# The recurrent branch's output product by Strassen's algorithm, in two groups of two pairs

## The chip, the cores and the metric

One core of a Trainium2 chip runs the kernel. The metric is the device time of one execution in microseconds (us): of three runs before the change the median is 1410.3, the lowest 1408.74 and the highest 1410.36. Engines are named as in the profile: PE (TensorE, matmuls), DVE (VectorE), ACT (ScalarE), POOL (GpSimd), SP (the queue that issues most loads).

## The reference

A decoder layer on 1024 tokens of 1024 channels in float32. Two mixers read one normalised input through one projection `z = u @ w_in`; their outputs are gated per channel and merged, and one more projection follows. The part around the change:

```python
y_pool = causal_multiscale_pool(z_pool, pool_w[i], pool_scale[i]) @ pool_proj[i]      # 512 -> 1024
y_lru = rglru_branch(z_lru, z_gelu, ...) @ lru_proj[i]                                # 1024 -> 1024
gates = jax.nn.sigmoid(z_gate.reshape(B, S, N_BRANCHES, D_MODEL) + b_gate[i])
merged = gates[:, :, 0, :] * y_pool + gates[:, :, 1, :] * y_lru
h = h + merged @ w_out[i]
```

Behind it come a SwiGLU block (`w_ffn_in`, `w_ffn_out`), a gated embedding and a last norm.

## The kernel before, in words

Everything is kept transposed: a tile has 128 channels on the partitions and 1024 tokens along the row, and a tensor of 1024 channels is eight such tiles. All stay in one pool of 51 buffers of SBUF (`at`, tag "a"); what doesn't fit goes through DRAM and comes back (`spill`, `store` on the POOL queue, loads on SP).

*Precision.* A float32 operand is made of two parts, a high one that ACT casts (`hi`, L115) and the low rest that DVE subtracts (`lo`, L119), each 128x512. A product of two operands takes three matmuls: high x high, high x low, low x high. `mm3` (L215) does this for one bank of 512 tokens, `mm6` (L223) for both banks of 1024 tokens with one weight.

*Two ways to multiply.* `plain` (L840) takes a block of 128 output channels after another: per output tile eight blocks of 128 inputs, two banks, three matmuls, 48 in all, in units of four input blocks (24 matmuls). `strassen` (L419) takes the output tiles in pairs and halves both the tokens and the channels: seven products of a pair (`PRODUCT`, L50, in the order `QS`, L417), each a unit of four input blocks by three matmuls (12), on sums of weights (`PairOf.operand`, L187: S1 to S4, DVE at L194) and on sums of activations (`Acts.run`, L386: operands B11, T1, T2, B21, T3, B22, T4 of each pair of input tiles; differences on DVE at L400 to L406). `Plain` (L484) adds the products of a pair up into two tiles z: ACT copies those of 1, 5, 6 and 4, DVE adds 2, 7 and 3. The input projection and the SwiGLU block's two products go by `strassen` before the change, the other products by `plain`.

*Order.* All engines follow the order in which the program is written. `drive` (L276) goes through the units: it runs the drain of the unit before (`post`), prepares weights three units ahead (cast, then low half), calls the unit's `pre`, lets `run_background` (L242) do some of the waiting generators (two at a time, by rough costs that they yield), and emits the unit's matmuls. What is written later on an engine waits behind what is written earlier.

*The stages here.* Pooling's product (`w_pproj`, four input blocks, 24 matmuls a tile) starts when the last tile of the recurrent branch, `y`, is stored; its drain `done_pproj` (L910) multiplies the first gate into each of eight tiles `t0`, which stay in SBUF. Beside it each of the eight y tiles comes back from DRAM and is split into operands (`reload`, L880). Then the recurrent product (`w_lru`, `plain` with the first two tiles' halves interleaved): `done_lru` (L930) multiplies the second gate into a tile, adds `t0` and splits the sum into operands `m`, one tile after every 48 matmuls. The output projection (`w_out`) follows, with the first norm's spreading (L367) ahead of it.

Of the kernel before, what the change touches and what calls it, by code (L numbers as in the profile page):

```python
# [19 lines left out]
KD = D // P  # L20
# [5 lines left out]
NH = 8  # L26
# [38 lines left out]
def hybrid_block(ctx: ExitStack, tc: tile.TileContext, xT, pT, vec, w_in, w_rgig, w_pool,  # L65
                 w_pproj, w_lru, w_out, w_fin, w_fout, w_pg, w_pp, outT):
    nc = tc.nc
# [8 lines left out]
    def at(name, dt=F32):  # L76
        return ap_.tile([P, T], dt, name=name, tag="a", bufs=NA)
# [4 lines left out]
    def spill(name):  # L82
        return dp.tile([P, T], F32, name=name, tag=name)
# [3 lines left out]
    def store(out, x):  # L87
        pool.dma_start(out, x)
# [32 lines left out]
    def split(x, name):  # L121

        ops = at(name, F32R), at(name, F32R)
        for op, s in zip(ops, (LOW, HIGH)):
            hi(op, x[:, s])
        for op, s in zip(ops, (LOW, HIGH)):
            lo(op, x[:, s])
        return ops
# [128 lines left out]
    def force(*keys):  # L257

        while any(k not in have for k in keys):
            assert background or inserted, keys  # L260
            for g in list(background)[:2]:
                step(g)
            while inserted:
                u = inserted.popleft()
                u.emit()
                u.post()
# [606 lines left out]
    t0 = {}  # L873
    gate_of = {}

    def load_gate(i):
        gate_of[i] = at("g")
        nc.sync.dma_start(gate_of[i], g_spill[i])

    def reload(src, into, key, name):  # L880
        x = at(name)
        nc.sync.dma_start(x, src)
        yield None
        yield None
        ops = into[key] = at(name, F32R), at(name, F32R)
        hi(ops[0], x[:, LOW])
        hi(ops[1], x[:, HIGH])
        yield None
        lo(ops[0], x[:, LOW])
        lo(ops[1], x[:, HIGH])  # L890
        have.add((name, "op", key))
        yield 1.4

    def begin_mixed():

        while "free" not in have or any(("mx", g) not in have for g in range(NG)):
            yield None
        for gi in range(NG):
            background.append(reload(m_spill[gi], mixed, gi, "mx"))
        load_gate(0)  # L900

    def pre_pproj(m, a):
        if m == 0:
            force(*[("y", c) for c in range(NH)], *[("mx", "op", g) for g in range(NG)])
            for c in range(NH):
                background.append(reload(y_spill[c], ys, c, "y"))
        if m + 1 < KD:
            load_gate(m + 1)

    def done_pproj(m, banks):  # L910
        g = gate_of.pop(m)
        for b, s in zip(banks, (LOW, HIGH)):
            dve.tensor_mul(g[:, s], g[:, s], b)
        t0[m] = g

    plain([w_pproj[m] for m in range(KD)], NG, lambda: mixed, done_pproj, pre_pproj)


    ms = {}

    def pre_lru(m, a):
        if m == 0 and a == 0:
            force(*[("y", "op", c) for c in range(4)])
            load_gate(8)
        if m == 0 and a == 4:
            force(*[("y", "op", c) for c in range(4, NH)])
        if a == 0 and m + 1 < KD:
            load_gate(8 + m + 1)

    def done_lru(m, banks):  # L930
        g = gate_of.pop(8 + m)
        for b, s in zip(banks, (LOW, HIGH)):
            dve.tensor_mul(g[:, s], g[:, s], b)
        dve.tensor_add(g, g, t0.pop(m))
        ms[m] = split(g, "m")

    plain([w_lru[m] for m in range(KD)], KD, lambda: ys, done_lru, pre_lru, 2)


    h_spill = [spill(f"h{m}") for m in range(KD)]  # L940
# [33 lines left out]
                state["norm2"] = Rstd(state["ss2"])  # L974
        return then

    plain([w_out[m] for m in range(KD)], KD, lambda: ms, lambda m, banks: residual(m)(banks), pre_out, 2)


    f_spill = [spill(f"f{j}") for j in range(NJ)]  # L980
# [207 lines left out]
    for p, s in enumerate((LOW, HIGH)):  # L1188
        for m in range(KD - NHOLD, KD):
# [27 lines left out]
            def pre(p=p, m=m):  # L1217
                if p == 0 and m + 1 < KD:
                    load_e(m + 1)
# [55 lines left out]
```

## Time and profile before

| | |
|---|---|
| median of three runs | 1410.3 us |
| the profiled execution's own time | 1409.52 us |
| its span | 1407.8 us |
| TensorE's mean granted clock in it | 0.986 |
| TensorE, VectorE, ScalarE, GpSimd busy | 97, 73, 48, 6% of the span |

The span runs from the first to the last instruction; the execution's own time adds what lies around it. Shares are averages over all stages; where a stage's limit lies is read from the rows of that stage.

### The profile page before, as it was taken

The page shows a single profiled execution, that of the slowest core. Times are in us where ns is not written, and L with a number is a line of the kernel's source. Part 1 is how long each engine was busy: PE and PEld are TensorE (multiplying, and loading weights), DVE is VectorE, ACT ScalarE, POOL GpSimd, SP SyncE. Part 2 cuts the span into 40 slices and gives each one's busy share as a digit, 9 for nine tenths or more (in the row PEclk, how much of TensorE's full clock was granted, in tenths as well). Part 3 has the DMA queues.
Part 4 walks back from the last instruction along what each step waited for, and adds up shares of the span by engine and source line. Part 5 has one row for each costly group of instructions (what it writes and reads, how often), then busy time and mean ns, then how long its engine had stood idle before and what let it go on. Part 6 is the DMA issues. An engine that isn't in the chain of part 4 may idle for free.

```text
span 1407.8 us, 16468 instructions
## 1 busy us (share of the span) xinstructions
PE 1364.6 (97%) x6006; PEld 1121.5 (80%) x6006; DVE 1032.6 (73%) x1523; ACT 675.3 (48%) x1074; POOL 86.5 (6%) x194
## 2 busy tenths in 40 slices
PE   6999999999999999999999999999999999999986
PEld 4787888888788888888888888888888877887865
DVE  5977788888785544566798888888878767768566
ACT  6558665887867112323554444444454422126331
POOL 0003010010000000000001000010110100000000
PEclk8999999999999999999999999999999999999997
DMA  7122143332549224231134334444577798813203
GB/s 315 75 79 95 61 155 111 115 134 99 200 162 400 89 75 147 105 125 43 60 115 152 132 143 148 150 149 165 194 266 269 295 419 303 326 64 120 72 19 120
DMA packets 64737, 220.55 MB, mean 157 GB/s; under 512 B 7312, under 2 KB 9872, under 8 KB 64656
## 3 DMA queue, kind: packets, MB, share of 16 engines
q1 hardware_dynamic: 45936, 151.80, 30.2%
q0 software_dynamic: 18576, 67.64, 11.9%
q8 instruction: 47, 0.77, 0.2%
q14 instruction: 34, 0.28, 0.1%
q10 hardware_dynamic: 144, 0.06, 0.0%
HBM read 147.65 MB, written 71.83 MB: 156 GB/s over the span
## 4 chain that ended last, share of the span: by engine, by line
PE 85%; DVE 6%; ACT 4%; issue 3%; DMA 1%; POOL 1%; DVEq 0%; SPq 0%; ACTq 0%; POOLq 0%
PE ps L221 22%; PE ps L219 22%; PE ps L220 22%; PE ps L227 17%; DVE w L119 1%; DVE ss L328 1%; DMA lT<-fT 1%; PE ps L367 1%; PE ps L345 1%; DVE pg L1139 0%; ACT pg L1137 0%; DVE h L1140 0%; ACT sq L1145 0%; DVE pg L1136 0%; DMA x<-xT 0%
## 5 line engine op out<-in xcount | busy, mean ns | idle before, releaser
L115 ACT CAST w<-wr 128x512 fp32r<-128x512 f32 (+2 forms) x376 | 221.6, 608 | 339.9 <-DVE wr L194 245.0
L119 DVE TENSOR_TENSOR w<-wr,w 128x512 fp32r<-128x512 f32 (+2 forms) x376 | 249.9, 671 | 44.2 <-ACT w L115 43.4
L221 PE MATMUL ps<-xT,w 128*128 128x512 f32 x640 | 249.5, 390 | 1.5 <-DVE w L119 1.4
L219 PE MATMUL ps<-xT,w 128*128 128x512 f32 x640 | 249.4, 390 | 0.1
L220 PE MATMUL ps<-xT,w 128*128 128x512 f32 x640 | 249.1, 389 | 0.0
L219 PE MATMUL ps<-xB,w 128*128 128x512 f32 x480 | 187.2, 390 | 2.1 <-ACT xB L115 1.2
L220 PE MATMUL ps<-xB,w 128*128 128x512 f32 x480 | 187.4, 391 | 1.9 <-DVE xB L119 1.9
L221 PE MATMUL ps<-xB,w 128*128 128x512 f32 x480 | 187.4, 390 | 0.0
L221 PEld LDWEIGHTS ps<-xT,w 128*128 128x128 f32 x640 | 120.1, 188 | 28.1 <-DVE w L119 3.2
L219 PEld LDWEIGHTS ps<-xT,w 128*128 128x128 f32 x640 | 120.2, 188 | 25.1 <-ACT w L115 0.5
L220 PEld LDWEIGHTS ps<-xT,w 128*128 128x128 f32 x640 | 120.1, 188 | 25.1
L220 PEld LDWEIGHTS ps<-xB,w 128*128 128x128 f32 x480 | 90.3, 188 | 21.8 <-DVE xB L119 3.1
L219 PEld LDWEIGHTS ps<-xB,w 128*128 128x128 f32 x480 | 90.2, 188 | 21.5 <-ACT xB L115 1.6
L221 PEld LDWEIGHTS ps<-xB,w 128*128 128x128 f32 x480 | 90.3, 188 | 19.2 <-DVE w L119 0.6
L227 PE MATMUL ps<-m,w 128*128 128x512 f32 x384 | 87.3, 389 | 0.0
L227 PE MATMUL ps<-y,w 128*128 128x512 f32 x384 | 87.2, 389 | 0.0
L227 PEld LDWEIGHTS ps<-y,w 128*128 128x128 f32 x384 | 72.1, 188 | 15.0
L227 PEld LDWEIGHTS ps<-m,w 128*128 128x128 f32 x384 | 72.0, 188 | 14.9
L1068 DVE TENSOR_TENSOR h<-h,ps 128x512 f32<-128x512 f32 x68 | 46.5, 684 | 42.5 <-PE ps L221 42.4
L194 DVE TENSOR_TENSOR wr<-wr 128x512 f32<-128x512 f32 (+1 forms) x104 | 70.4, 678 | 3.0 <-DMA wr<-w_fout 1.2
L219 PE MATMUL ps<-lT,w 128*128 128x512 f32 x176 | 69.0, 392 | 3.4 <-DMA lT<-fT 2.7
L221 PE MATMUL ps<-lT,w 128*128 128x512 f32 x176 | 68.7, 390 | 0.0
(214 smaller groups left out, 2190.3 us busy)
## 6 DMA issues: line engine op xcount, KB each, us to landing
wr<-w_fin SPq DMA_DIRECT2D x44, 512.0 KB, 5.6
fT<-xT POOLq DMA_DIRECT2D x44, 512.0 KB, 5.0
lT<-fT SPq DMA_DIRECT2D x44, 512.0 KB, 7.9
wr<-w_in SPq DMA_DIRECT2D x36, 512.0 KB, 4.3
fB<-xB POOLq DMA_DIRECT2D x33, 512.0 KB, 5.8
lB<-fB SPq DMA_DIRECT2D x33, 512.0 KB, 6.7
g<-z POOLq DMA_DIRECT2D x16, 512.0 KB, 2.9
g<-g SPq DMA_DIRECT2D x16, 512.0 KB, 6.4
```

The lines of the kernel that those rows point to most:

```text
L115: act.copy(op[:, :x.shape[1]], x)
L119: dve.tensor_tensor(op[:, H:H + n], x, op[:, :n].bitcast(F32), ALU.subtract)
L194: f(self.place(out), self.place(a), self.place(b))
L219: pe.matmul(bank, a, xop[:, :H], start=first, stop=False, skip_group_check=more)
L220: pe.matmul(bank, a, xop[:, H:], start=False, stop=False, skip_group_check=more)
L221: pe.matmul(bank, b, xop[:, :H], start=False, stop=last, skip_group_check=more)
L227: pe.matmul(bank, w, xop[:, s], start=f, stop=e)
L328: dve.tensor_add(ss, ss, sq)
L345: pe.matmul(m[:, i:i + 1], self.ss[:, t:t + P], mean, start=True, stop=last is None)
L367: pe.matmul(bank[:, i * P:(i + 1) * P], r[:, b + i:b + i + 1].broadcast_to([P, P]), ident, start=True, stop=True)
L1068: dve.tensor_add(h[t][:, s], h[t][:, s], bank)
```

## The change

- The recurrent product goes by `strassen`, four pairs of output tiles in two groups of two, with the weights' rows paired on the host (`pairs`).
- y comes back in pairs of tiles (`reload_pair`), and five of its seven operands are made in the background, beside pooling's product; B22 and T4 are made in the first group by `prepare_y`.
- Pooling's gated tiles are stored to DRAM (`t_spill`) and loaded again, with the second gates, at the third to sixth product of each group (`gates_of_group`).
- `merge` multiplies the gate into the whole tile z, adds t and splits the sum. It runs as soon as a pair's tile is complete: after its product 3 for the even tile, after its product 4 for the odd one.
- `w_out` takes its inputs in the order 0, 1, 2, 3, 4, 6, 5, 7.

```diff
@@ -891,6 +891,17 @@
         have.add((name, "op", key))
         yield 1.4
 
+    ya = Acts()
+
+    def reload_pair(k):
+        t = at("y"), at("y")
+        for i in (0, 1):
+            nc.sync.dma_start(t[i], y_spill[2 * k + i])
+        yield None
+        yield None
+        ya.a[k], ya.b[k] = t
+        yield from some_operands(ya, k, ORDER[:5])
+
     def begin_mixed():
 
         while "free" not in have or any(("mx", g) not in have for g in range(NG)):
@@ -902,8 +913,8 @@
     def pre_pproj(m, a):
         if m == 0:
             force(*[("y", c) for c in range(NH)], *[("mx", "op", g) for g in range(NG)])
-            for c in range(NH):
-                background.append(reload(y_spill[c], ys, c, "y"))
+            for k in range(NH // 2):
+                background.append(reload_pair(k))
         if m + 1 < KD:
             load_gate(m + 1)
 
@@ -911,30 +922,44 @@
         g = gate_of.pop(m)
         for b, s in zip(banks, (LOW, HIGH)):
             dve.tensor_mul(g[:, s], g[:, s], b)
-        t0[m] = g
+        store(t_spill[m], g)
+
+    t_spill = [spill(f"t{m}") for m in range(KD)]
 
     plain([w_pproj[m] for m in range(KD)], NG, lambda: mixed, done_pproj, pre_pproj)
 
 
     ms = {}
 
-    def pre_lru(m, a):
-        if m == 0 and a == 0:
-            force(*[("y", "op", c) for c in range(4)])
-            load_gate(8)
-        if m == 0 and a == 4:
-            force(*[("y", "op", c) for c in range(4, NH)])
-        if a == 0 and m + 1 < KD:
-            load_gate(8 + m + 1)
-
-    def done_lru(m, banks):
-        g = gate_of.pop(8 + m)
-        for b, s in zip(banks, (LOW, HIGH)):
-            dve.tensor_mul(g[:, s], g[:, s], b)
-        dve.tensor_add(g, g, t0.pop(m))
-        ms[m] = split(g, "m")
-
-    plain([w_lru[m] for m in range(KD)], KD, lambda: ys, done_lru, pre_lru, 2)
+    prepare_y = prepare(ya)
+
+    def gates_of_group(m0):
+        def pre(q, j, size):
+            i = QS.index(q)
+            if m0 == 0:
+                if i == 0 and j == 0:
+                    while len(ya.b) < NH // 2:
+                        for g in list(background)[:2]:
+                            step(g)
+                prepare_y(q, j, size)
+            if j == 0 and i in (2, 3, 4, 5):
+                m = m0 + {2: 0, 3: 2, 4: 1, 5: 3}[i]
+                load_gate(8 + m)
+                t0[m] = at("t")
+                nc.sync.dma_start(t0[m], t_spill[m])
+        return pre
+
+    def merge(m):
+        def then(z):
+            g = gate_of.pop(8 + m)
+            dve.tensor_mul(g, g, z)
+            dve.tensor_add(g, g, t0.pop(m))
+            ms[m] = split(g, "m")
+        return then
+
+    strassen(ya, [(w_lru[2 * i], w_lru[2 * i + 1]) for i in range(KD // 2)],
+             lambda i: Plain(merge(2 * i), merge(2 * i + 1)), gates_of_group(0),
+             last=gates_of_group(4), groups=[2, 2])
 
 
     h_spill = [spill(f"h{m}") for m in range(KD)]
@@ -974,7 +999,8 @@
                 state["norm2"] = Rstd(state["ss2"])
         return then
 
-    plain([w_out[m] for m in range(KD)], KD, lambda: ms, lambda m, banks: residual(m)(banks), pre_out, 2)
+    plain([w_out[m] for m in range(KD)], KD, lambda: ms, lambda m, banks: residual(m)(banks), pre_out, 2,
+          (0, 1, 2, 3, 4, 6, 5, 7))
 
 
     f_spill = [spill(f"f{j}") for j in range(NJ)]
@@ -1256,7 +1282,7 @@
-        "w_lru": tiles(a["lru_proj"][0]),
+        "w_lru": tiles(pairs(a["lru_proj"][0])),
```

Three places of the order. In the names, xB and xT are operands of y, w a weight's operand, wr the weight as loaded (its sums are made in place), s the sum S2, z a product's tile, g a gate, t pooling's gated tile, m an operand of `w_out`.

VectorE at the seam, before: the last drain of pooling's product, the rest of y's low halves, the first drain of the recurrent product.

```order
L913 TENSOR_TENSOR g<-g,ps 128x512 x2
L119 TENSOR_TENSOR w<-wr,w 128x512 x2
L119 TENSOR_TENSOR y<-y 128x512 x4
L119 TENSOR_TENSOR w<-wr,w 128x512
L119 TENSOR_TENSOR y<-y 128x512 x4
L933 TENSOR_TENSOR g<-g,ps 128x512 x2
L934 TENSOR_TENSOR g<-g 128x1024
L119 TENSOR_TENSOR m<-g,m 128x512 x2
L119 TENSOR_TENSOR w<-wr,w 128x512
```

The first multiply of the merge (L933) has only y's low halves and weights ahead of it. VectorE there now, from the same last drain; the first xB in these rows belongs to the third pair of y.

```order
L924 TENSOR_TENSOR g<-g,ps 128x512 x2
L119 TENSOR_TENSOR w<-wr,w 128x512
L194 TENSOR_TENSOR s_3929<-wr 128x512
L119 TENSOR_TENSOR xT_3895<-y,xT_3895 128x512
L119 TENSOR_TENSOR xT_3897<-y,xT_3897 128x512
L119 TENSOR_TENSOR xB_3943<-y,xB_3943 128x512
L119 TENSOR_TENSOR xB_3945<-y,xB_3945 128x512
L400 TENSOR_TENSOR y<-y 128x512
L119 TENSOR_TENSOR w<-s_3929,w 128x512
L194 TENSOR_TENSOR s_3929<-wr 128x512
L400 TENSOR_TENSOR y<-y 128x512
L119 TENSOR_TENSOR xT_3950<-y,xT_3950 128x512
```

Where eight plain low halves of y followed the drain, S2's difference and the operands of a product now do; the third and fourth B11 (the two xB) stand behind the last drain and behind S2's difference. ScalarE at the same place, its casts of these operands:

```order
L115 CAST xT_3897<-y 128x512
L115 CAST w<-s_3929 128x512
L115 CAST xB_3943<-y 128x512
L115 CAST xB_3945<-y 128x512
L115 CAST xT_3950<-y 128x512
L497 COPY z<-ps 128x512
```

S2's cast, which reads the difference, has come to stand ahead of the casts of the third and fourth B11.

VectorE at the end of the first group: from the differences of T4 to the third merge.

```order
L406 TENSOR_TENSOR y<-y 128x512 x2
L119 TENSOR_TENSOR xT_4183<-y,xT_4183 128x512
L406 TENSOR_TENSOR y<-y 128x512
L503 TENSOR_TENSOR z<-z,ps 128x512
L955 TENSOR_TENSOR g<-g,z 128x1024
L956 TENSOR_TENSOR g<-g,t 128x1024
L119 TENSOR_TENSOR m<-g,m 128x512 x2
L119 TENSOR_TENSOR w<-wr,w 128x512
L119 TENSOR_TENSOR xT_4186<-y,xT_4186 128x512
L406 TENSOR_TENSOR y<-y 128x512
L119 TENSOR_TENSOR xT_4190<-y,xT_4190 128x512
L119 TENSOR_TENSOR xT_4224<-y,xT_4224 128x512
```

The first merge (L955, L956, m) stands ahead of T4's last three operands.

VectorE behind it, from the second merge to the third and the low half of a weight:

```order
L503 TENSOR_TENSOR z<-z,ps 128x512
L955 TENSOR_TENSOR g<-g,z 128x1024
L956 TENSOR_TENSOR g<-g,t 128x1024
L119 TENSOR_TENSOR m<-g,m 128x512 x2
L119 TENSOR_TENSOR w<-wr,w 128x512
L194 TENSOR_TENSOR wr<-wr 128x512 x2
L955 TENSOR_TENSOR g<-g,z 128x1024
L956 TENSOR_TENSOR g<-g,t 128x1024
L119 TENSOR_TENSOR m<-g,m 128x512 x2
L119 TENSOR_TENSOR w<-wr,w 128x512
```

One weight's low half and one weight's two sums now stand between two merges; before, 48 matmuls of TensorE lay between two. ScalarE at the same place, in its casts of m and of weights:

```order
L115 CAST m<-g 128x512 x2
L115 CAST w<-wr 128x512
L509 COPY z<-ps 128x512
L115 CAST m<-g 128x512 x2
L115 CAST w<-wr 128x512
L509 COPY z<-ps 128x512
L115 CAST m<-g 128x512 x2
```

The cast of the weight's sum stands ahead of the copy of product 4 (L509), and that copy ahead of the cast of m.

## Rows read from the trace of the kernel before

**Rows 1.** The page's first lines: busy us (share of the span) and instructions.

```profile
span 1407.8 us, 16468 instructions
...
PE 1364.6 (97%) x6006; PEld 1121.5 (80%) x6006; DVE 1032.6 (73%) x1523; ACT 675.3 (48%) x1074; POOL 86.5 (6%) x194
```

**Rows 2.** Chain that ended last, 380 to 700 us: start us, us, what.

```profile
429.03 130.56 PE ps L227 x576
559.59 1.78 PE ps L367 x16
561.38 87.08 PE ps L227 x384
```

**Rows 3.** By stage: busy us of PE, PEld, DVE, ACT, POOL; clock, DMA share, GB/s.

```profile
385.00:425.00 40.00, 39.63 (x175) 32.58 (x174) 30.15 (x45) 27.14 (x43) 1.59 (x3) 1.00 0.53 186
429.00:472.60 43.60, 43.60 (x194) 36.10 (x193) 24.78 (x37) 24.24 (x38) 2.23 (x5) 1.00 0.70 276
472.60:559.60 87.00, 87.00 (x386) 72.06 (x385) 42.32 (x62) 14.77 (x27) 0.00 (x0) 1.00 0.32 109
```

**Rows 4.** Waits, 420 to 660 us: us in total, times, longest us.

```profile
DVE g L933 <- PE ps L227: 39.4, 8, 8.4
```

**Rows 5.** Timeline of VectorE, 470 to 494 us: start us, us, operation, [idle before].

```profile
472.37 1.28 DVE L913 TENSOR_TENSOR g<-g,ps 128x512 f32<-128x512 f32 x2 [3.56 <-PE ps L227]
473.57 1.29 DVE L119 TENSOR_TENSOR w<-wr,w 128x512 fp32r<-128x512 f32 x2
474.77 2.49 DVE L119 TENSOR_TENSOR y<-y 128x512 fp32r<-128x512 f32 x4
477.18 0.68 DVE L119 TENSOR_TENSOR w<-wr,w 128x512 fp32r<-128x512 f32 x1
...
488.69 1.28 DVE L933 TENSOR_TENSOR g<-g,ps 128x512 f32<-128x512 f32 x2 [8.42 <-PE ps L227]
490.00 1.23 DVE L934 TENSOR_TENSOR g<-g 128x1024 f32<-128x1024 f32 x1
491.97 1.29 DVE L119 TENSOR_TENSOR m<-g,m 128x512 fp32r<-128x512 f32 x2 [0.74 <-ACT m L115]
493.18 0.69 DVE L119 TENSOR_TENSOR w<-wr,w 128x512 fp32r<-128x512 f32 x1
```

**Rows 6.** Timeline of ScalarE, pieces from 425 to 500 us.

```profile
434.71 0.58 ACT L509 COPY z<-ps 128x512 f32<-128x512 f32 x1
...
440.11 2.17 ACT L115 CAST y<-y 128x512 fp32r<-128x512 f32 x4
...
491.32 1.15 ACT L115 CAST m<-g 128x512 fp32r<-128x512 f32 x2 [22.41 <-DVE g L934]
492.37 0.62 ACT L115 CAST w<-wr 128x512 fp32r<-128x512 f32 x1
```

**Rows 7.** As rows 3, of stretches in and after stops of TensorE.

```profile
36.00:40.00 4.00, 2.18 (x7) 1.23 (x8) 3.86 (x6) 1.24 (x2) 0.00 (x0) 1.00 0.32 131
40.00:44.00 4.00, 4.00 (x12) 3.09 (x12) 3.93 (x7) 0.62 (x1) 0.00 (x0) 0.58 0.00 0
1390.00:1392.00 2.00, 0.00 (x0) 0.00 (x0) 1.38 (x2) 0.53 (x1) 0.00 (x0) 0.92 0.00 0
1392.00:1394.00 2.00, 1.24 (x6) 1.25 (x7) 0.00 (x0) 1.91 (x2) 0.00 (x0) 0.50 0.00 0
```

**Rows 8.** Chain that ended last, 36 to 46 us.

```profile
39.75 0.62 PE ps L220
40.37 0.43 PE ps L221
...
43.66 0.23 PE ps L220
```

**Rows 9.** DMA issues: operation, count, KB each, median us to landing.

```profile
g<-z POOLq DMA_DIRECT2D x16, 512.0 KB, 2.9
g<-g SPq DMA_DIRECT2D x16, 512.0 KB, 6.4
...
wr<-w_lru SPq DMA_DIRECT2D x8, 512.0 KB, 6.9
```

## Prediction

> **What bounds the kernel now.** I read the page's busy times first: TensorE is busy for 1364.6 of 1407.8 us, VectorE for 1032.6 [rows 1]. The reader should not stop there, since 97% is an average. Next comes the chain that ended last, from pooling's product on: 576 matmuls follow each other without a piece between them, 130.56 us, so **0.2267 us for one**, then 1.78 us of the norm's spreading, then 384 more [rows 2]. Of these 576, 192 are pooling's product (429.0 to 472.6 us) and 384 the recurrent branch's (472.6 to 559.6). By stage, TensorE is busy in every microsecond of both; VectorE has 24.78 of 43.6 and 42.32 of 87.0 us to do, ScalarE 24.24 and 14.77 [rows 3]. The waits agree: the drains of the recurrent product wait for TensorE, 39.4 us in eight times [rows 4]. So TensorE bounds this place, and VectorE has about half its time free. A matmul saved here is worth 0.2267 us as long as VectorE stays ahead of TensorE, and that is what the change uses up.
>
> **Prices.** A VectorE operation on 128x512 (call it a half) takes 0.68 us alone, 0.60 in a row: four take 2.49 [rows 5]. One on 128x1024 takes 1.23 and starts 0.03 after the one whose result it reads [rows 5]. A ScalarE cast takes 0.62, 0.52 in a row (four: 2.17), a copy from a bank 0.58 [rows 6]. The turn from VectorE to ScalarE and back costs VectorE 0.74 us of idleness at every merged tile [rows 5], for the cast starts 0.09 us behind the sum (490.00 + 1.23, then 491.32) and lasts 0.62 [rows 5, 6].
>
> **What is removed.** Four pairs of output tiles by seven products of 4 x 3 matmuls are 336 instead of 384: 48 x 0.2267 = **10.9 us less** on TensorE, all of it on the path. The Trainium skill (TensorE: Matmul & The Clock Gate, Back-to-back issue gap) gives about 131 ns for a 512-column matmul in a sustained stream; by that the saving would be 6.3 us. The trace disagrees with it, 0.2267 us here, and the row decides.
>
> **What is added.** VectorE gets 60 instructions more: 44 instead of 16 for the operands of y (per pair of tiles seven low halves and four differences), 44 instead of 16 for the weights, and 28 instead of 24 in the drains and merges. That is 28 + 28 halves and 7.2 us of wider drains, about 41 us of work. Pooling's product covers 14 halves of y and four differences of weights, 10.8 us, where eight halves of y stood: 24.78 + 6.0 us in 43.6. This costs nothing; without that cover it would stand ahead of the first product. The other 35 us come on top of 42.32 in a stage that should last 28 units of 12 matmuls, 76.2 us: by the sum alone VectorE is full there, so it matters where its queue is late.
>
> *The seam.* The third and fourth operand B11 stand in VectorE's queue behind the last drain of pooling's product, which can't start before 472.37 [rows 5]. Behind it come two drains, one weight half and the difference S2: 3 x 0.60 + 0.68 = 2.48, so 474.85. ScalarE casts S2 first (0.09 + 0.52) and then the third B11 (0.62): 476.1. VectorE subtracts: 476.8, and the fourth 477.4. TensorE started the first product at 472.6 and wants their low halves with its 8th and 11th matmul, at 474.2 and 474.9. It stops for **2.6 us** in all. Before, the second four tiles of y had two units of 24 matmuls between the seam and their use.
>
> *The merges of the first group.* This is the larger stop. From the end of the 11th of the 28 units (the first S4 product, 12 matmuls or 2.72 us each) VectorE's queue holds, in this order: the drain of the first tile and its merge, a weight, the rest of operand T4, drain and merge of the second tile, a weight and two differences, the third merge, a weight and two differences, the fourth merge, and the low half of the second S1. Priced:
> - a merge: 1.26 + 1.23 + 0.74 + 1.20 = 4.43; before, the like took 488.69 to 493.18, 4.49 [rows 5]; two of the four have a drain of 0.71 ahead: 4 x 4.43 + 1.42 = 19.1
> - the rest of T4, four halves of which the last waits for a difference and its cast: 0.60 + 1.42 + 0.60 = 2.6
> - the weight 0.60; then twice a weight, two differences of which the second reads the first, and a turn by ScalarE that casts the weight and only then copies the bank that the next merge reads: 0.60 + 0.71 + 0.68 + 0.09 + 0.52 + 0.65 = 3.25, so 6.5
> - the last low half 0.68
>
> In all 29.5 us. It starts 1.5 us behind the unit's end, since 4.2 us of such work stand behind the unit before. TensorE has 6 units and 2 matmuls to do meanwhile, 16.8 us, and then needs that last low half. So it waits 29.5 + 1.5 - 16.8, **14.2 us**, in three stops: on T4's last three operands (5 us), the first S1's low half (4), the second's (5).
>
> *After that* VectorE recovers. The last group has the same four merges, with four weights 21.5 us from its S4 product's end; but w_out takes the eighth tile 3 units, 1.8 us of spreading and 15 us of its own matmuls later, 25 us. Hidden, and the new order of w_out's sum gives the tiles in the order in which they are made.
>
> *The clock.* The trace shows what a stop can do: between 36 and 40 us TensorE is busy 2.18 of 4 us, and in the next four the granted clock is 0.58; near the end it is idle from 1390 to 1392 and then at 0.50, the 1.2 GHz level [rows 7]. In the first of these places nine steps took 39.75 to 43.66, 3.91 us where 2.04 would do: 1.9 us lost [rows 8]. The last two stops are 4 and 5 us with 2.3 us of work between. I take one fall, **1.9 us**, behind the last stop; falls at the earlier ones only shorten the stop after them, since VectorE sets its end. Bounds: 0, and two that count, 3.8.
>
> *Transfers.* Eight stores of 0.5 MB join the POOL queue beside pooling's product and eight loads the SP queue. Gate and t tile of the first merge are asked for six units, 16 us, ahead of their use; a gate lands in 6.4 us, weights of this product in 6.9, a stored gate in 2.9 [rows 9], and the DMA engines are at 0.32 in that stage [rows 3]. Nothing, then; the upper bound is one landing of 6.9 that is not covered, as behind the SP queue's load of t2, which waits for the store of t7 with the second group's weights behind it. ScalarE's 40 added casts and copies, 21 us, fit beside its 14.77 of 87.
>
> **Sum.** -10.9 + 2.6 + 14.2 + 1.9 = **+7.8 us**. The profiled execution took 1409.52 us around its span of 1407.8; the median of the runs, 1410.3, is 0.8 above it. On the median: **1418.1**. With the seam at 2.1 to 3.1, the chain 1.5 us either way and the clock at 0 to 3.8, the case itself reaches from +3.9 to +11.7: 1414.2 to 1422.0.
>
> The Trainium skill (VectorE: DVE Perf Modes, The DRAIN you can't avoid) says that the next operation doesn't start until the pipeline has emptied. By that each half would cost 0.68 and the chain some 1.5 us more, 1419.6. The trace has 2.49 for four, so the row's 0.60 stands.
>
> **Rivals.**
> 1. *VectorE runs the merges without gaps* (not slower). The same instructions at their pace in a row, eight wide ones at 1.20 and 22 halves at 0.60, are 22.8 instead of 29.5 us; TensorE then waits 7.5, its gaps are short and the clock stays, and the sum is -10.9 + 2.6 + 7.5 = -0.8: 1409.5. The point is a chain of 23.6 us. For it: in the input projection, also by Strassen's algorithm, VectorE is 30.15 of 40 us busy and TensorE hardly misses a beat, 39.63 [rows 3]. Against it: the idle 0.74 us stand in the trace inside each merge [rows 5]. 0.14.
> 2. *The stops are only the seam's*: VectorE comes to the first merge so far ahead, 14 us, that the merges pass while TensorE works. -10.9 + 2.6: 1402.0. The input projection speaks for it as well; but no merge stands in its stream, and VectorE can't be ahead of a product that it drains. 0.05.
> 3. *The clock doesn't fall*: +5.9, 1416.2. For it: between 36 and 40 us it still stands at 1.00 with TensorE idle for nearly half the time [rows 7]. 0.18.
> 4. *A transfer is late on top*, 6.9: 1425.0. 0.05.
>
> My forecast has 0.58. The range takes the case's own bounds and reaches down to the first rival, 1409.4 to 1422.0, which leaves out rivals 2 and 4, 0.10. About 0.2%, 2.8 us, is what a measurement can tell from no change. Slower by more: 0.58 + 0.18 + 0.05 = 0.81; within: most of rival 1, 0.09; faster: rival 2 and the rest of 1, 0.10.
>
> **What would show it.** Right: TensorE has three idle places of 4 to 5 us in the second half of this stage, ended by VectorE (an operand T4, then weights of line 119), and one of some 2 us at its start; the stage lasts about 95 us instead of 87; the clock is below 1.00 in it once; w_out's stage is as long as before. Wrong: a stage of 76 to 80 us; or waits there that a DMA ends; or time lost outside it.

## The result, and the profile after

The changed kernel takes **1419.24 us** (median of four runs, 1418.91 to 1420.89) beside 1410.33 of the kernel before on the same chip: a ratio of 1.0059, 95% interval 1.0044 to 1.0075, **8.9 us slower** by the medians (their quotient is 1.0063, inside the interval). The profiled execution took 1418.91 us around a span of 1416.8. The forecast was 1418.1 in a range of 1409.4 to 1422.0.

The page's first lines answer to [rows 1]: 48 matmuls fewer, 60 VectorE instructions more.

```profile
span 1416.8 us, 16536 instructions
...
PE 1360.5 (96%) x5958; PEld 1115.2 (79%) x5958; DVE 1075.1 (76%) x1583; ACT 697.8 (49%) x1114; POOL 91.0 (6%) x202
```

TensorE saves only 4.1 us of busy time, where 48 x 0.2267 are 10.9: a matmul at the lower clock counts as busy for longer (0.63 us instead of 0.39 from 477.66 to 480.22 us, with starts 0.427 us apart instead of 0.2267). The chain that ended last, behind the stage, answers to [rows 2]:

```profile
569.70 1.78 PE ps L367 x16
571.49 87.08 PE ps L227 x384
```

The spreading (L367) started at 559.59 before and now at 569.70; `w_out`'s 384 matmuls last 87.08 us in both. From pooling's first matmul (428.87 before, 429.19 now) to the spreading it was 130.72 us and is 140.51: **9.8 us more in this stage**. What lies behind it takes 848.2 us before and 847.1 now, a difference that two executions of one kernel show as well (the repeat of the changed kernel, below, has 848.7). The stage in two windows, columns as in [rows 3]:

```profile
429.40:472.90 43.50, 43.50 (x193) 36.03 (x192) 30.83 (x47) 19.43 (x29) 5.96 (x12) 1.00 0.79 321
472.90:569.70 96.80, 83.71 (x338) 66.78 (x338) 71.57 (x104) 37.61 (x68) 0.53 (x1) 0.93 0.44 153
```

Pooling's product covers 6.05 us more of VectorE's work (30.83, it was 24.78) and costs TensorE nothing: 43.50 of 43.50. The recurrent product lasts 96.80 us. Its 336 matmuls would take 336 x 0.2267 = 76.2; so 20.6 us are lost: 13.1 of stops (96.80 less 83.71) and 7.5 with TensorE busy for longer than its matmuls need at 0.2267. Most of the 7.5 is the lower clock (mean 0.93 of full speed). Some is not: with the clock at 1.00 throughout, the same product still keeps TensorE busy for 77.68 us (experiment 5). TensorE's waits from 460 to 580 us name the stops (us in total, times, longest):

```profile
PE ps L221 <- DVE w L119: 6.3, 2, 3.3
PE ps L220 <- DVE xT L119: 4.4, 1, 4.4
PE ps L219 <- ACT xB L115: 2.2, 1, 2.2
PE ps L220 <- DVE xB L119: 0.2, 1, 0.2
```

The two xB are the third and fourth operand B11 at the seam, xT is operand T4, and w are the two weights S1 of the second group, 3.3 and 3.0 us. No stop is ended by a DMA. VectorE's timeline shows what stood ahead of T4 and of S1 (start us, us, operation, [idle before]):

```profile
508.99 0.68 DVE L503 TENSOR_TENSOR z<-z,ps 128x512 f32<-128x512 f32 x1
509.70 1.22 DVE L955 TENSOR_TENSOR g<-g,z 128x1024 f32<-128x1024 f32 x1
510.96 1.23 DVE L956 TENSOR_TENSOR g<-g,t 128x1024 f32<-128x1024 f32 x1
512.87 1.29 DVE L119 TENSOR_TENSOR m<-g,m 128x512 fp32r<-128x512 f32 x2 [0.68 <-ACT m L115]
514.08 0.68 DVE L119 TENSOR_TENSOR w<-wr,w 128x512 fp32r<-128x512 f32 x1
514.69 0.68 DVE L119 TENSOR_TENSOR xT<-y,xT 128x512 fp32r<-128x512 f32 x1
...
525.61 1.23 DVE L955 TENSOR_TENSOR g<-g,z 128x1024 f32<-128x1024 f32 x1 [1.17 <-ACT z L509]
...
533.23 1.23 DVE L955 TENSOR_TENSOR g<-g,z 128x1024 f32<-128x1024 f32 x1 [1.17 <-ACT z L509]
...
537.61 0.68 DVE L119 TENSOR_TENSOR w<-wr,w 128x512 fp32r<-128x512 f32 x1
```

The first merge (509.70 to 514.08) stands between the drain of its tile (L503) and T4's rest. The whole chain, from that drain's start to the end of the second S1's low half at 538.29, is 29.30 us. The clock fell behind the seam and three times around the chain, as windows show:

```profile
472.00:480.00 8.00, 5.56 (x18) 3.93 (x17) 7.26 (x12) 2.78 (x6) 0.53 (x1) 0.83 0.64 234
480.00:490.00 10.00, 10.00 (x43) 8.20 (x43) 7.46 (x13) 6.12 (x12) 0.00 (x0) 0.96 0.32 107
...
515.00:520.00 5.00, 4.58 (x14) 3.60 (x15) 4.79 (x7) 0.62 (x1) 0.00 (x0) 0.67 0.01 3
520.00:525.00 5.00, 5.00 (x24) 4.13 (x23) 3.72 (x6) 1.67 (x4) 0.00 (x0) 1.00 0.00 0
525.00:530.00 5.00, 2.50 (x12) 1.73 (x10) 3.62 (x4) 1.72 (x4) 0.00 (x0) 1.00 0.00 0
530.00:535.00 5.00, 4.21 (x12) 3.06 (x12) 3.76 (x6) 1.10 (x2) 0.00 (x0) 0.69 0.00 0
535.00:540.00 5.00, 2.01 (x6) 1.32 (x6) 3.58 (x6) 2.16 (x4) 0.00 (x0) 0.84 0.61 219
540.00:545.00 5.00, 5.00 (x19) 4.03 (x18) 3.32 (x6) 3.72 (x8) 0.00 (x0) 0.78 0.76 258
```

It is below 1.00 behind each of the four stops: the seam's, T4's, and the two on S1 (0.69 to 0.84 and 0.78).

### The profile page after: what moved, and what is told of

It is laid out like the page before. It is cut to its first block, busy times and chain, and to the rows that moved or that the text cites. A ratio compares the mean times of both kernels' runs of the same rounds, so it can differ in the third digit from the quotient of the medians.

```text
span 1416.8 us, 16536 instructions
## 1 busy us (share of the span) xinstructions
PE 1360.5 (96%) x5958; PEld 1115.2 (79%) x5958; DVE 1075.1 (76%) x1583; ACT 697.8 (49%) x1114; POOL 91.0 (6%) x202
## 4 chain that ended last, share of the span: by engine, by line
PE 75%; DVE 11%; DMA 4%; ACT 4%; issue 4%; POOL 1%; DVEq 0%; SPq 0%; ACTq 0%; POOLq 0%
PE ps L221 21%; PE ps L220 21%; PE ps L219 21%; PE ps L227 11%; DMA lT<-fT 2%; DVE w L119 2%; DVE wr L194 1%; DVE ss L328 1%; DMA fB<-xB 1%; DMA hr<-h 1%; PE ps L367 1%; DVE xB L119 1%; PE ps L345 1%; DVE pg L1165 1%; DVE h L1166 0%
## 5 line engine op out<-in xcount | busy, mean ns | idle before, releaser
L115 ACT CAST w<-wr 128x512 fp32r<-128x512 f32 (+2 forms) x384 | 227.2, 609 | 356.0 <-DVE wr L194 259.6
L119 DVE TENSOR_TENSOR w<-wr,w 128x512 fp32r<-128x512 f32 (+2 forms) x384 | 256.2, 672 | 47.1 <-ACT w L115 46.4
L221 PE MATMUL ps<-xT,w 128*128 128x512 f32 x704 | 276.1, 392 | 7.8 <-DVE w L119 7.7
L220 PE MATMUL ps<-xT,w 128*128 128x512 f32 x704 | 276.1, 392 | 4.4 <-DVE xT L119 4.4
L219 PE MATMUL ps<-xT,w 128*128 128x512 f32 x704 | 276.0, 392 | 0.1
L219 PE MATMUL ps<-xB,w 128*128 128x512 f32 x528 | 206.5, 391 | 4.4 <-ACT xB L115 3.4
L220 PE MATMUL ps<-xB,w 128*128 128x512 f32 x528 | 206.8, 392 | 2.1 <-DVE xB L119 2.1
L221 PE MATMUL ps<-xB,w 128*128 128x512 f32 x528 | 206.7, 391 | 0.0
L221 PEld LDWEIGHTS ps<-xT,w 128*128 128x128 f32 x704 | 133.2, 189 | 38.3 <-DVE w L119 10.6
L220 PEld LDWEIGHTS ps<-xT,w 128*128 128x128 f32 x704 | 133.2, 189 | 32.6 <-DVE xT L119 5.1
L219 PEld LDWEIGHTS ps<-xT,w 128*128 128x128 f32 x704 | 133.1, 189 | 28.2 <-ACT w L115 0.7
L219 PEld LDWEIGHTS ps<-xB,w 128*128 128x128 f32 x528 | 99.6, 189 | 26.2 <-ACT xB L115 4.3
L220 PEld LDWEIGHTS ps<-xB,w 128*128 128x128 f32 x528 | 99.5, 188 | 24.4 <-DVE xB L119 3.9
L221 PEld LDWEIGHTS ps<-xB,w 128*128 128x128 f32 x528 | 99.7, 189 | 21.2 <-DVE w L119 0.6
L227 PE MATMUL ps<-m,w 128*128 128x512 f32 x384 | 87.3, 389 | 0.0
L227 PEld LDWEIGHTS ps<-m,w 128*128 128x128 f32 x384 | 72.0, 188 | 14.9
L194 DVE TENSOR_TENSOR wr<-wr 128x512 f32<-128x512 f32 (+1 forms) x112 | 76.0, 679 | 3.1 <-DMA wr<-w_fout 1.1
L219 PE MATMUL ps<-lT,w 128*128 128x512 f32 x176 | 69.1, 392 | 3.2 <-DMA lT<-fT 3.0
L221 PE MATMUL ps<-lT,w 128*128 128x512 f32 x176 | 68.7, 390 | 0.0
L220 PE MATMUL ps<-lT,w 128*128 128x512 f32 x176 | 68.5, 389 | 0.0
L115 ACT CAST w<-s 128x512 fp32r<-128x512 f32 (+1 forms) x56 | 34.3, 613 | 53.5 <-DVE s L194 53.5
```

The lines of the kernel that those rows point to most:

```text
L115: act.copy(op[:, :x.shape[1]], x)
L119: dve.tensor_tensor(op[:, H:H + n], x, op[:, :n].bitcast(F32), ALU.subtract)
L194: f(self.place(out), self.place(a), self.place(b))
L219: pe.matmul(bank, a, xop[:, :H], start=first, stop=False, skip_group_check=more)
L220: pe.matmul(bank, a, xop[:, H:], start=False, stop=False, skip_group_check=more)
L221: pe.matmul(bank, b, xop[:, :H], start=False, stop=last, skip_group_check=more)
```

## The experiments

*The theory* before them: the place of the four merges in VectorE's queue makes TensorE wait for T4 and S1, the order of y's operands makes it wait at the seam, and the stops take the clock down. *Rivals*: VectorE simply has too much to do; each stop and each fall of the clock is a loss of its own; t's trip through DRAM. Eight edited kernels ran, three of them a second time, and the change itself again. "Stage" is the time from pooling's first matmul (L227) to the first norm's spreading (L367) in each one's profile; it is what the experiments touch, and a second profile of the same kernel agreed within 0.4 us in all four cases. (The recorded expectations count the stage some 0.2 us shorter.) The gains over the change are up to 2.1 us smaller in the whole than in the stage, and the time behind the stage, 846.5 to 850.2 us over all profiles, is too uneven to say where that goes. So the readings rest on the stage.

| | median us | before, same chip | ratio (95%) | stage us |
|---|---|---|---|---|
| kernel before | | | | 130.72 |
| the change | 1419.24 | 1410.33 | 1.0059 (1.0044 to 1.0075) | 140.51 |
| 1 merges deferred | 1406.73 | 1412.16 | 0.9962 (0.9948 to 0.9975) | 125.36 |
| 2 T4 ahead of the first merge | 1419.43 | 1412.16 | 1.0060 (1.0047 to 1.0072) | 140.48 |
| 3 B11 first | 1419.00 | 1412.16 | 1.0050 (1.0037 to 1.0063) | 137.35 |
| 4 stops filled | 1416.59 | 1412.16 | 1.0036 (1.0023 to 1.0048) | 137.29 |
| 5 deferred, and B11 first | 1404.59 | 1410.82 | 0.9954 (0.9942 to 0.9966) | 122.09 |
| 6 four t kept in SBUF | 1421.06 | 1410.82 | 1.0069 (1.0058 to 1.0081) | 140.51 |
| 7 `w_out` in the old order | 1420.92 | 1410.82 | 1.0068 (1.0054 to 1.0081) | 140.58 |
| 8 low halves later | 1413.27 | 1410.82 | 1.0016 (1.0007 to 1.0025) | 133.80 |
| the change again | 1419.46 | 1410.53 | 1.0064 (1.0052 to 1.0076) | 140.89 |
| 1 again | 1405.73 | 1410.53 | 0.9964 (0.9952 to 0.9976) | 125.31 |
| 3 again | 1417.58 | 1410.53 | 1.0052 (1.0038 to 1.0066) | 137.32 |
| 5 again | 1402.72 | 1410.53 | 0.9946 (0.9934 to 0.9957) | 122.09 |

### 1: the merges deferred

```diff
+    def late_merge(m, z):
+        g = gate_of.pop(8 + m)
+        dve.tensor_mul(g, g, z)
+        yield 1.2
+        dve.tensor_add(g, g, t0.pop(m))
+        ops = at("m", F32R), at("m", F32R)
+        hi(ops[0], g[:, LOW])
+        hi(ops[1], g[:, HIGH])
+        yield 1.2
+        yield None
+        lo(ops[0], g[:, LOW])
+        lo(ops[1], g[:, HIGH])
+        ms[m] = ops
+        yield 1.2
+
     def merge(m):
         def then(z):
+            if m < 4:
+                background.append(late_merge(m, z))
+                return
...
+                while any(i not in ms for i in range(4)):
+                    for g in list(background)[:2]:
+                        step(g)
```

> The first group's four merges become background work: T4's last operands and the weights S1 come ahead of them in VectorE's queue, and the merges' steps are spread over the second group. The same work is done. My theory (the place of the merges in VectorE's queue makes TensorE stop, and the stops make the clock fall): the stops on T4 and on the two S1 weights go (4.4 + 3.3 + 3.0 us to 1 us at most each) with the clock's falls behind them; the stop at the seam stays (2.4 us and some 2 us at the lower clock). 336 matmuls x 0.2267 = 76.2 us and 4 to 6 on top: a stage of 80 to 82 us instead of 96.8, and 1402 to 1405.5 us in all. Rival, VectorE's load as such: with some 35 us of work more in this stage VectorE is full, the deferred merges come up as waits in the second group or ahead of w_out, and the time stays within 4 us of 1419. Rival, a transfer (t through DRAM): the stops stay at the merges' new places.

Measured: 0.9962, **13.7 us below the change** by the two ratios and 5.4 below the kernel before. All waits of TensorE in the stage:

```profile
PE ps L219 <- ACT xB L115: 2.2, 1, 2.2
PE ps L220 <- DVE xB L119: 0.2, 1, 0.2
PE ps L220 <- DVE xT L119: 0.2, 1, 0.2
```

The seam's stop is as it was, those on S1 are gone, and 0.2 us are left on T4. VectorE has no less to do:

```profile
520.00:525.00 5.00, 5.00 (x24) 4.14 (x23) 4.97 (x8) 1.36 (x4) 0.00 (x0) 1.00 0.00 0
525.00:530.00 5.00, 5.00 (x24) 4.14 (x23) 5.00 (x8) 3.57 (x8) 0.00 (x0) 1.00 0.43 136
530.00:535.00 5.00, 5.00 (x24) 4.14 (x23) 5.00 (x8) 3.27 (x7) 0.00 (x0) 1.00 0.83 277
```

It is busy in every microsecond here (third pair of numbers: 4.97, 5.00, 5.00 of 5), and TensorE too. So it was the order of the queue and not the load; that rival falls. The edit does two things to the order: it moves the merges back, and it puts other work between a merged tile's high and low halves, so that VectorE doesn't wait for ScalarE's cast there. The second thing is tried alone in experiment 8.

### 2: T4 ahead of the first merge, the rest as in the change

```diff
                 prepare_y(q, j, size)
+                while held:
+                    now, z = held.pop()
+                    now(z)
...
+    held = []
+
     def merge(m):
-        def then(z):
+        def now(z):
...
+        def then(z):
+            if m == 0:
+                held.append((now, z))
+            else:
+                now(z)
```

> Only the first merge changes its place with T4's last three operands; all the rest stays in the order of the change. My theory (one VectorE chain of 29 us sets the end of the last stop, and what it does first doesn't matter): the stop on T4 goes from 4.4 us to under 1, the two stops on S1 grow by about as much, from 6.3 to some 10 us, and the time stays at 1419, 1.5 us either way. Rival, each stop is a loss of its own: 4.4 us of stop and 1 to 2 us of lower clock behind it come back, 1413 to 1415.

Measured: 1.0060 and a stage of 140.48 us, the change to within 0.03. The waits from 500 to 545 us:

```profile
PE ps L221 <- DVE w L119: 8.8, 3, 3.5
PE ps L220 <- DVE xT L119: 0.2, 1, 0.2
```

The stop of 4.4 us on T4 is 0.2 now; in its place stands a third one on a weight, 3.5. One chain sets the end, and which of these two pieces it does first doesn't matter. That each stop is a loss of its own is false here.

### 3: the B11 of all four pairs first

```diff
         ya.a[k], ya.b[k] = t
-        yield from some_operands(ya, k, ORDER[:5])
+        yield from some_operands(ya, k, ORDER[:1])
+        background.append(some_operands(ya, k, ORDER[1:5]))
```

> Only the order of y's operands in the background changes: the B11 of all four pairs are made first, then T1 to T3 of each. My theory: the stop at the seam (2.2 + 0.2 us) goes and the clock doesn't fall behind it (some 2 us), and since VectorE's chain of merges starts from the 11th unit's end, all of it comes forward: 1414.2 to 1416.5 us. Rival, the later stops swallow it (their ends are set by VectorE alone): 1419, the stops on T4 and S1 being longer by 4 us in sum. Rival, the next operands (T1) are late instead: a stop of 1 to 3 us on T1 in the units behind, 1417 to 1419.

The stage is 3.2 us shorter, and in its first profile the stop at the seam is gone and the clock at 1.00 until the merges. The waits from 429 to 575 us:

```profile
PE ps L221 <- DVE w L119: 6.3, 2, 4.6
PE ps L220 <- DVE xT L119: 5.1, 2, 4.8
```

The chain of merges starts 76.52 us after pooling's first matmul instead of 79.80. Not all of the seam's cost comes forward: VectorE is busy for 9.86 of the ten us from 480 on, and TensorE stops for 0.37 on an operand there. The times agreed less well: 1.3 us by the ratios (1417.4 where the kernel before takes 1410.3), outside the expected 1414.2 to 1416.5, and in this profile what lies behind the stage took 850.0 us, 2.9 more than in the change's. So it was run again:

> The third experiment again. Its profile had this stage 3.2 us shorter than the change's (137.2 against 140.3), its times only 0.0009 of ratio, 1.3 us. Theory (the seam's stop and its clock are worth 3.2 us): 3.2 us below the change on the same chip, 1 us either way. Rival (what is gained here is lost behind this stage): 1.5 us or less, and a stage behind it that is longer by some 2 us.

1.9 us below the change on the same chip, between theory and rival, the stage again 3.2 us shorter than in the first profile of the change. The intervals of the two ratios (0.0028 and 0.0024 wide) overlap and separate 1.9 neither from 3.2 nor from nothing; what lies behind the stage takes 848.7 us, as in the repeat of the change, so the rival's longer stage behind didn't come back. The gain is shown in the stage, twice; in the whole it was 1.3 and 1.9 us, not clear of noise.

### 4: the stops filled

```diff
...
                 for k in range(nk):
+                    if warmed is not None and (where, q, j, k) in warmed:
+                        if (i, "W") not in banks:
+                            banks[i, "W"] = ps()
+                        for _ in range(warmed[where, q, j, k]):
+                            pe.matmul(banks[i, "W"], warm[:, :P], warm, start=True, stop=True)
...
+             warmed={(0, 1, 0, 2): 9, (0, 4, 0, 1): 17, (1, 5, 0, 0): 13, (1, 5, 1, 0): 11}
```

> At the four places where TensorE stops, 9, 17, 13 and 11 products of a constant tile are put ahead of the waiting matmul, into a bank that nothing reads: TensorE is busy through most of each stop, and all else is as in the change. My theory: the clock stays at 1.00 or near it through the stage; what falls at the seam (some 2 us) and behind the last stop (some 1.5 us) cost comes back, what the falls in between cost does not, since VectorE sets the ends of the later stops: 1414.5 to 1417 us, the stops and the products in them taking some 16 us. Rival, every fall is a loss of its own: the 7.5 us that the stage lasts beyond 76.2 us of matmuls and 13.1 of stops all come back, 1411 to 1413. Rival, the clock doesn't depend on the stops: 1419 or some tenths more.

Measured: 3.2 us less in the stage and 1.0036, 3.2 us less by the ratios. The clock stays up while TensorE still idles for some of the time:

```profile
520.00:530.00 10.00, 9.10 (x40) 6.09 (x40) 7.33 (x11) 3.39 (x6) 0.00 (x0) 1.00 0.00 0
530.00:540.00 10.00, 7.58 (x32) 4.98 (x33) 7.33 (x11) 3.35 (x6) 0.00 (x0) 1.00 0.37 114
```

And VectorE's chain didn't notice. Its first and last instruction in this run:

```profile
508.49 0.68 DVE L508 TENSOR_TENSOR z<-z,ps 128x512 f32<-128x512 f32 x1
...
537.11 0.68 DVE L119 TENSOR_TENSOR w<-wr,w 128x512 fp32r<-128x512 f32 x1
```

537.79 - 508.49 = 29.30 us, to the hundredth what it was with the clock falling. So the falls between the stops cost nothing: of the 7.5 us by which TensorE was busy for longer, 3.2 came back, and what the falls between the stops had cost had only shortened the stops. The table cuts each stage at the chain: up to its first instruction, the chain, and from its end to the spreading.

| | up to the chain | chain | behind it |
|---|---|---|---|
| the change | 79.80 | 29.30 | 31.41 |
| the change again | 79.81 | 29.30 | 31.78 |
| 2 T4 first | 79.81 | 29.28 | 31.39 |
| 3 B11 first | 76.52 | 29.41 | 31.42 |
| 4 stops filled | 78.19 | 29.30 | 29.80 |
| 8 low halves later | 79.80 | 22.58 | 31.42 |

With the clock up it is 1.6 us less ahead of the chain (the seam's fall) and 1.6 behind it (the last one's), and nothing between.

### 5: both

The edits of 1 and 3 together.

> The merges of the first group as background work (as in the first experiment) and the B11 of all four pairs first (as in the third), together. My theory: the two causes add. The merges' part gave 13.7 us by the ratios (0.9962 against 1.0059), of the seam's stop 2.4 us and some 2 us of lower clock are left in it, and nothing behind sets an end of its own now: 3 to 4.5 us less than the first experiment, a ratio to the kernel before of 0.9930 to 0.9942 (1400.5 to 1402.1 where that one takes 1410.3), with the clock at 1.00 through the whole stage. Rival, as in the third experiment, where VectorE handed on only a part: it is full behind the seam, T4 and S1 come late again, and 1 to 2 us less than the first experiment is all: 0.9948 to 0.9955.

The first time 0.9954, only 1.1 us below the first experiment by the ratios; the rival had that. But the stage was 3.3 us shorter, so both were run again on one chip, and the change with them:

> The change itself again, on the same chip as the three that follow: 1.0045 to 1.0070 of the kernel before, with the stage from pooling's first matmul to the norm's spreading at 140.3 us, as in its first profile.

> The first experiment again: 0.9948 to 0.9975 of the kernel before, the stage at 125.2 us.

> The fifth experiment again. Its profile had this stage 3.3 us shorter than that of the merges deferred alone (121.9 against 125.2), its times 0.0008 of ratio, 1.1 us. Theory: 3.3 us below it on the same chip, 1 us either way, the fastest of the four, at 0.9930 to 0.9950 of the kernel before. Rival, as in the run before this one: 1.5 us or less below it.

On that chip: the change 1419.46, the merges deferred 1405.73, both 1402.72. **3.0 us below the first experiment, 16.7 below the change and 7.8 below the kernel before** (0.9946, 0.9934 to 0.9957): the fastest version. The intervals of this and of the first experiment just overlap (0.9957 and 0.9952); that the two differ rests on their stages, 3.3 and 3.2 us apart in two pairs of profiles. All waits of TensorE and the recurrent product of its second profile:

```profile
PE ps L220 <- DVE xT L119: 0.8, 3, 0.4
```

```profile
472.50:551.00 78.50, 77.68 (x339) 62.70 (x338) 72.25 (x109) 39.10 (x72) 0.53 (x1) 1.00 0.56 194
```

The causes add in the stage (125.36 to 122.09). VectorE is busy for 72.25 of 78.5 us, 92%, and TensorE waits for 0.8: that much work fits, if it is in the right order.

The repeat of the change shows something of its own. In its profile the clock stays up through the first S1 stop and falls later:

```profile
530.00:535.00 5.00, 2.88 (x12) 2.17 (x12) 3.63 (x6) 1.76 (x4) 0.00 (x0) 1.00 0.00 0
535.00:540.00 5.00, 0.46 (x2) 0.32 (x2) 4.28 (x6) 1.14 (x2) 0.00 (x0) 0.71 0.70 210
540.00:545.00 5.00, 5.00 (x15) 3.92 (x15) 2.91 (x5) 3.75 (x8) 0.00 (x0) 0.61 0.62 193
```

The second stop on S1 is 4.5 us there instead of 3.0, since TensorE came to it sooner, and the chain is 29.30 us again: the fall between the two stops had only been taken out of the stop.

### 6: four of t's tiles kept in SBUF

```diff
-        store(t_spill[m], g)
+        if m < 4:
+            t0[m] = g
+        else:
+            store(t_spill[m], g)
...
-                t0[m] = at("t")
-                nc.sync.dma_start(t0[m], t_spill[m])
+                if m >= 4:
+                    t0[m] = at("t")
+                    nc.sync.dma_start(t0[m], t_spill[m])
```

> As the change, but pooling's first four gated tiles stay in SBUF: four stores and four loads of 0.5 MB less, and no trip through DRAM for the four merges at which TensorE stops. My theory (transfers cost nothing here): the same stops and 1419, 1.5 us either way, a ratio to the kernel before of 1.0045 to 1.0070. Rival, the loads of t set the start of merges: the stop on T4 shrinks or goes, 1414 or less.

Measured: 1.0069 and a stage of 140.51 us, that of the change to the hundredth, with the same four stops. The trip of these four tiles through DRAM costs nothing; keeping them gives nothing. (That more than four can be kept wasn't tried.)

### 7: `w_out` in the old order

```diff
-    plain([w_out[m] for m in range(KD)], KD, lambda: ms, lambda m, banks: residual(m)(banks), pre_out, 2,
-          (0, 1, 2, 3, 4, 6, 5, 7))
+    plain([w_out[m] for m in range(KD)], KD, lambda: ms, lambda m, banks: residual(m)(banks), pre_out, 2)
```

> As the change, but w_out takes its inputs in the order 0 to 7 as before. My theory: nothing, since all eight tiles are made by 582.4 us, which is when the second half of w_out's inputs is first wanted: 1419, 1.5 us either way, with no stop of TensorE in w_out. Rival: the fifth tile, made after the sixth, holds up w_out by up to one merge, 4.4 us: 1421 to 1424.

Measured: 1.0068; `w_out`'s 384 matmuls run without a break, as in the change:

```profile
572.69 87.08 PE ps L227 x384
```

The new order is worth nothing here.

### 8: the merged tile's low halves later

```diff
                 prepare_y(q, j, size)
+            while held:
+                lo(*held.pop(0))
...
-            ms[m] = split(g, "m")
+            if m >= 4:
+                ms[m] = split(g, "m")
+                return
+            ms[m] = at("m", F32R), at("m", F32R)
+            for op, s in zip(ms[m], (LOW, HIGH)):
+                hi(op, g[:, s])
+                held.append((op, g[:, s]))
```

> As the change, but in the first group's merges VectorE makes the low halves of a merged tile only behind the next weight's operations, so that it doesn't stand idle while ScalarE casts the high ones; the number of operations is the same. My theory (29.3 us of one chain of VectorE set the end): the four idle pieces of some 0.7 us go, 2.8 us, and the last pair of low halves comes behind the last weight S1 instead of ahead of it, 1.2 us: the chain is 25.3 us and the time 1414.5 to 1416.5, the stop on T4 2.5 us and those on S1 some 4. Rival, TensorE and ScalarE (the copies of product 4, the casts of weights) set the pace of that stretch and the idle pieces come back at another place: less than 1.5 us.

Measured: 1.0016, 6.1 us below the change by the ratios, and 6.7 in the stage, more than I expected. VectorE at the second and third merge:

```profile
520.53 1.22 DVE L960 TENSOR_TENSOR g<-g,t 128x1024 f32<-128x1024 f32 x1
521.67 0.69 DVE L119 TENSOR_TENSOR w<-wr,w 128x512 fp32r<-128x512 f32 x1
522.27 1.41 DVE L194 TENSOR_TENSOR wr<-wr 128x512 f32<-128x512 f32 x2
523.61 1.29 DVE L119 TENSOR_TENSOR m<-g,m 128x512 fp32r<-128x512 f32 x2
524.90 1.22 DVE L959 TENSOR_TENSOR g<-g,z 128x1024 f32<-128x1024 f32 x1
```

There is no idle piece left: the two waits of 1.17 us for ScalarE's copy of product 4 went as well, since the low halves fill them. The chain is 22.58 us instead of 29.30, 6.72 less (1.2 of it the last two low halves, which now come behind its end), and the stage 6.71 less: microsecond for microsecond, the chain is what the kernel waits for. Of the 15.2 us that the first experiment took off the stage, so much can be had without moving the merges.

## Why the prediction was right

The forecast of +7.8 us met +8.9 (stage: +9.8). By its steps:

- **The saving, 10.9 us**: as priced. With next to nothing in its way the recurrent product takes 78.5 us (experiment 5) for 76.2 of matmuls. What is left are three short waits, 0.8 us in sum, and single steps of about 0.3 us behind them and early in the product; the others are still 0.2267.
- **The cover of pooling's product**: as said, 30.83 us of VectorE for the 30.8 expected, and TensorE without a gap.
- **The seam, 2.6 us**: the idle time is 2.4 us, for the reason given (the third B11 behind S2's difference and its cast). ScalarE there:

```profile
475.26 0.62 ACT L115 CAST w<-s 128x512 fp32r<-128x512 f32 x1 [3.10 <-DVE s L194]
475.79 1.13 ACT L115 CAST xB<-y 128x512 fp32r<-128x512 f32 x2
```

  But the step is mis-sized in the whole: the 11th unit ended at 507.26, and from pooling's first matmul at 429.19, 192 + 132 matmuls and 2.6 us would give 505.2. The seam cost 4.6 us; of the two that are missing most are the clock (1.6 by experiment 4).
- **The merges, 14.2 us**: the chain was priced at 29.5 us and is 29.30. It started 1.73 us behind the 11th unit's end where 1.5 was said, and ended at 538.29, 31.03 behind it; less TensorE's 16.8 that is 14.2. Its parts are not as forecast: stops of 4.4, 3.3 and 3.0 us instead of 5, 4 and 5, and the other 3.5 us are TensorE's longer steps inside the chain's time, most of them at the lower clock.
- **The clock, 1.9 us**: I took one fall, behind the last stop; there it cost 1.6 (1.98 in the repeat). It fell four times. "Falls at the earlier ones only shorten the stop after them" holds for the falls between the merges' stops (experiment 4, and the repeat) and **is the step that failed for the seam's**: VectorE doesn't run on its own there. Behind the seam it still waits for TensorE, for the last time ahead of the merges at the first drain of product 2:

```profile
496.58 0.69 DVE L499 TENSOR_TENSOR z<-z,ps 128x512 f32<-128x512 f32 x1 [1.89 <-PE ps L221]
```

  From there VectorE's queue runs up to the merges and through them with no further wait for TensorE, so a stop or a fall ahead of this place moves the whole chain (by 1.6 us in experiment 4, by 3.3 with the stop in experiment 3). 1.6 us were left out. The upper bound, two falls that count, is what came: 1.6 + 1.6 of its 3.8.
- **Transfers, 0**: as said (no stop ended by a DMA; experiment 6). **The last group and `w_out`**: hidden as said, with or without the new order (experiment 7).

Put together with what was measured: -10.9 + 4.6 + 14.2 + 1.6 = +9.5, beside +9.8 in the stage. That the whole came nearer to the forecast than the stage did is luck: of the two profiles compared, the changed kernel's has 1.1 us less behind the stage, which the change doesn't touch.

Rival 1, a chain of 22.8 us, was not what happened, but experiment 8 came to 22.58 us, with the idle pieces gone and two low halves less in the chain. Its sum said a wait of 7.5 us, and the chain's end is 24.3 us behind the 11th unit's (which, like the chain's start, lies as far behind pooling's first matmul as in the change), less 16.8: 7.5. It expected the clock to stay, though, and the seam's and the last fall cost 3.2 us: 1.0016 instead of no change. Rival 2 (only the seam) is the first experiment; it came to 0.9962, 1405 us, where the rival has 1402.0, since the seam costs 4.6 and not 2.6. Rival 3 (the clock doesn't fall) is the fourth: it gave 3.2 us, where 1.9 was counted. Rival 4 (a transfer) didn't occur.

The Trainium skill (TensorE: Matmul & The Clock Gate, Loop structure matters more than you think) has it that copying a result out of PSUM on VectorE doesn't break the clock's warmth, in a loop whose next matmuls follow immediately. The trace of the kernel before agrees, 1.00 through the stage [rows 3]. In the change the next matmuls don't follow immediately, and the clock was 0.67 and 0.69 behind the stops: the same engine that takes the results out makes the next operands, and drains and merges stood ahead of these in its queue.

## What to carry to other kernels

Faster arithmetic that saves matmuls pays only if the vector work it adds stands in the right place of an in-order queue: what the next matmul waits for goes ahead of what only a later stage reads. Price the chain from the end of the unit that its first drain reads to the operand that ends it, with the work that still stands ahead of that drain and the idle turns between engines, and compare it with TensorE's work in between; the difference was the loss here, and moving one item within the chain changed nothing. A fall of the clock cost time where TensorE set the pace, also ahead of such a chain, and nothing inside it.

## What was not expected of the hardware

- The clock fell behind stops of 2.2 and 0.2 us at the seam (0.83 of full speed from 472 to 480 us); I had priced a fall only behind 4 to 5 us. With products of a constant tile in the stops it stood at 1.00, though TensorE was busy for only 7.58 of the 10 us from 530 to 540.
- When it falls differs between executions of one kernel (0.69 from 530 to 535 us in one profile, 1.00 in the other), and the stage differs by 0.4 us.
- Two VectorE operations on 128x1024 of which the second reads the first start 1.26 us apart (509.70, 510.96); an operation that doesn't read such a result starts 1.14 us behind it (520.53 and 521.67 in experiment 8).
